# Last tile of an output projection summed from two banks, and two products of an up-projection made in halves of columns

## The chip, the core and the metric

The kernel is one program on one core of a Trainium2 chip. The metric is the device time of one execution in microseconds (us). TensorE (PE) multiplies matrices; VectorE (DVE), ScalarE (ACT) and GpSimd (POOL) work element by element; SyncE (SP) issues the transfers. Each engine has a queue of its own and works through it in order, and waits where an operand is not there yet. TensorE's results land in PSUM, which is cut into banks of 512 float32 columns.

## What is computed

One decoder layer, for 1024 tokens of width 1024, in float32:

```python
h = x * (1.0 + sc1) + sh1
proj = h @ w_in[l]
...                                    # two kinds of attention heads, fox and ret
mix = jnp.concatenate([fox, ret], axis=-1) @ w_out[l]
x = layer_norm(ALPHA * x + g1 * mix, ln1_g[l], ln1_b[l])
h = x * (1.0 + sc2) + sh2
u = causal_depthwise_conv(h @ w_up[l], conv_w[l], conv_b[l])
a, bv = jnp.split(u, 2, axis=-1)
y = (jax.nn.gelu(a, approximate=False) * bv) @ w_down[l]
x = layer_norm(ALPHA * x + g2 * y, ln2_g[l], ln2_b[l])
```

The change lies where the output projection (`w_out`) and its normalisation end and the up-projection (`w_up`, to 2 x 2816 columns) begins.

## The kernel before

Every float32 operand of a large product is kept as a high part (rounded to the format that TensorE reads) and a low part (the rest); a product of two of them is three matmuls: high by high, high by low, low by high (`three`, lines 189 to 191 in the output projection, and `three_w`, lines 1175 to 1177). A split is a cast on ScalarE and a subtraction on VectorE (`op_split_cols`, lines 874 and 875; `w_split`, lines 1124 and 1125).

**Output projection.** The tokens are 8 tiles of 128. For each tile `op_mm` makes 1024 output columns in two halves `n` of 512, from 8 pieces of 128 inputs in two calls (`m4` = 1 for the retention heads, then 0): 12 matmuls for each half and call. The result `op` is one tile of two banks (`bank2`). `op_end` then takes, half by half, `t = op * gate` (line 996) and `acc = ALPHA * x + t` with its row sum (line 997), then the mean (line 1002), the sum of squares on ScalarE (line 1007), its root, the reciprocal, and the normalisation on ScalarE (line 1011). `h2_turn` transposes a finished tile on TensorE (`nT`, line 890), and ScalarE scales it into `hr` (line 893). For the last tile, 7, `op_mm(NT - 1, 0, ...)` has the transposes of tile 6 in its middle, and `op_end` follows.

**Up-projection.** The tokens are parted into even and odd tiles, so that four tiles side by side are 512 columns, and the 1024 inputs into two halves. Of each block `ff` (22 of them, 128 + 128 output rows) 7 products are made in place of 8 (a Strassen-like scheme): products 1 to 7, each of 4 pieces of 128 by 512 columns, thus 12 matmuls. Their operands are `hr` itself and sums of parts of it, `t1` to `t4` (the tile name `ht` in the trace; `h` for the others), made by `h2_sums` (lines 915 to 920) and split by `h2_split`. Columns 0:128 belong to tiles 0 and 1, 128:256 to tiles 2 and 3, 256:384 to tiles 4 and 5, 384:512 to tiles 6 and 7. So the last 128 columns of every operand that mixes even and odd tiles wait for tile 7's normalisation, its transposes, the sums and the splits. The columns 0:384 of `t2` and `t1` are split ahead of that.

`up_12` makes products 1 and 2 (which read even tiles only), `up_657` products 6, 5 and 7, `up_43` products 4 and 3. Product 1 goes into a bank `uX`, is copied out (`u`, line 1190), and products 6, 7 and 4 are added on top in the same bank; product 6's running sum is copied as U2. Product 2 has one bank of `uY`, products 5 and 3 share the other. Weight operands are split as well: `wA` for products 1 and 2, `wS` for 5 and 6, `wD` for 7 and 4, `wZ` for 3. In the program's text the start of the stage reads:

```python
    with tc.issue_after(pins["norm"].ins), tc.issue_after(pins["bias"].ins):
        h2_split("t1", slice(0, 3 * P))
        up_12(0)
        w_s(0, "S")
        h2_turn(NT - 1)
        h2_low(NT - 1)
        for key in ("t2", "t1"):
            low = h2_split(key, slice(3 * P, 4 * P))
        with tc.issue_after(low.ins):
            up_12(1)
```

and then `up_657(0)`, with `up_43(0)` behind it.

**What sets the order.** The text is not the order of the queues. The block is planned when the program is built: of the instructions that are ready in the planner's own model of time, each engine takes the one that stands first in the text. `tc.issue_after(i)` adds that what is written under it comes behind instruction `i` on `i`'s engine. Tiles come out of rings: single banks out of a ring of four ("B"), two-bank tiles out of a ring of two ("A"). A tile that takes a ring's place waits until the one before it there has been read.

Of the kernel before, what the change touches and what calls it, by code (L numbers as in the profile page):

```python
# [8 lines left out]
F32 = mybir.dt.float32  # L9
# [6 lines left out]
P = 128  # L16
# [15 lines left out]
def kernel(  # L32
# [838 lines left out]

    def op_split_cols(key, c, src, sl):
        hi, lo = hop[key][0][c][:, :, sl], hop[key][1][c][:, :, sl]
        nc.scalar.copy(hi, src[:, :, sl])
        return nc.vector.tensor_tensor(out=lo, in0=src[:, :, sl], in1=f(hi), op=ALU.subtract)

    def h2_turn(i):
        n, q0 = i % 2, (i // 2) * P
        acc = accs[i]
        if i < 2:  # L880
            for jp in range(4):
                hr[jp, n] = slot("X", [P, 2, 512], F32, f"hr{jp}_{n}")
        if i == 0:
            op_tiles("11", "X")
            op_tiles("21", "X")
        for q in range(2):
            pt = bank(f"nT{i}_{q}")
            for b in range(4):
                j = 4 * q + b
                nc.tensor.transpose(pt[:, b * P:(b + 1) * P], acc[:, j * P:(j + 1) * P], ident)  # L890
            for b in range(4):
                j = 4 * q + b
                nc.scalar.activation(
                    hr[j // 2, n][:, j % 2, q0:q0 + P], pt[:, b * P:(b + 1) * P], AF.Identity,
                    scale=AB[:, 0, j:j + 1], bias=AB[:, 1, j:j + 1],
                )
            if n == 0:
# [10 lines left out]

    def h2_sums(sl):

        for c in range(2):
            op_split_cols("22", c, hr[2 + c, 1], sl)
            e1, o1 = hr[c, 0][:, :, sl], hr[c, 1][:, :, sl]
            e2, o2 = hr[2 + c, 0][:, :, sl], hr[2 + c, 1][:, :, sl]
            nc.vector.tensor_tensor(out=e1, in0=e1, in1=o1, op=ALU.subtract)
            nc.vector.scalar_tensor_tensor(
                out=o1, in0=o1, scalar=-1.0, in1=o2, op0=ALU.mult, op1=ALU.add)
            nc.vector.scalar_tensor_tensor(
                out=o2, in0=e1, scalar=-1.0, in1=o2, op0=ALU.mult, op1=ALU.subtract)
            nc.vector.scalar_tensor_tensor(  # L920
                out=e2, in0=o2, scalar=-1.0, in1=e2, op0=ALU.mult, op1=ALU.subtract)
# [3 lines left out]
    def h2_split(key, sl):  # L925
        jp, n = TOPS[key]
        if key not in hop:
            op_tiles(key, "H")
        for c in range(2):
            low = op_split_cols(key, c, hr[jp + c, n], sl)  # L930
        return low
# [46 lines left out]
    def op_mm(i, m4, mid=None):  # L978
        if m4 == 1:
            ops[i] = bank2(f"op{i}")  # L980
        s_ = mxs[i, m4]
        for n in range(2):
            sl = slice(n * 512, (n + 1) * 512)
            for m in range(4 * m4, 4 * m4 + 4):
                if mid is not None and n == 0 and m == 4 * m4 + 2:
                    mid()
                three(ops[i][:, sl], s_[:, 0, m % 4, :], s_[:, 1, m % 4, :],
                      wo[m][0][:, sl], wo[m][1][:, sl], m == 4, m == 3)

    def op_end(i):  # L990

        acc, t_ = accs[i], sos[i][:, 512:1024]
        sums = small([P, 2], f"osum{i}")
        for n in range(2):
            sl = slice(n * 512, (n + 1) * 512)
            nc.vector.tensor_tensor(out=t_, in0=ops[i][:, sl], in1=g_row[:, sl], op=ALU.mult)
            pins["sum"] = nc.vector.scalar_tensor_tensor(
                out=acc[:, sl], in0=acc[:, sl], scalar=ALPHA, in1=t_,
                op0=ALU.mult, op1=ALU.add, accum_out=sums[:, n:n + 1],
            )  # L1000
        nmu = small([P, 1], f"onm{i}")
        nc.vector.tensor_scalar(
            out=nmu, in0=sums[:, 0:1], scalar1=sums[:, 1:2], scalar2=-1.0 / D,
            op0=ALU.add, op1=ALU.mult,
        )
        r = small([P, 1], f"ors{i}")
        nc.scalar.activation(sos[i], acc, AF.Square, bias=nmu, accum_out=r)
        nc.scalar.activation(r, r, AF.Sqrt, scale=1.0 / D, bias=epsc)
        nc.vector.reciprocal(r, r)
# [84 lines left out]
    for i in range(NT - 1):  # L1094
        op_mm(i, 0)
        op_split(i + 1, 0)
        if i + 2 < NT:
            x_load(i + 2)
            op_load(i + 2)
            op_split(i + 2, 1)  # L1100
        op_end(i)
        if i > 0:
            h2_turn(i - 1)
            h2_low(i - 1)
            op_mm(i + 1, 1)

# [14 lines left out]
    def w_split(raw, tag, name):  # L1121
        hi = slot(tag, [P, ND, P], F32R, f"{name}h")
        lo = slot(tag, [P, ND, P], F32R, f"{name}l")
        nc.scalar.copy(hi, raw)
        nc.vector.tensor_tensor(out=lo, in0=raw, in1=f(hi), op=ALU.subtract)
        return [(hi[:, k:k + 4, :], lo[:, k:k + 4, :]) for k in (0, 4)]

# [16 lines left out]
    def w_d(ff, tag="X"):

        if ff < NFF:
            a, b = ra[ff], rb[ff]
            nc.vector.tensor_tensor(out=b[:, 0:4, :], in0=a[:, 0:4, :], in1=b[:, 0:4, :],
                                    op=ALU.add)
            W[ff, 7], W[ff, 4] = w_split(b, tag, f"wD{ff}")  # L1150

    def w_4(ff, tag="S"):

        if ff < NFF:
            a, s = ra[ff], rs[ff]
# [36 lines left out]

    def up_12(ff):
        if ff == NFF:
            return
        st = ups[ff] = {"X": bank(f"uX{ff}"), "YZ": bank2(f"uY{ff}")}
        y = st["YZ"][:, 0:512]
        prod(ff, 1, st["X"], True, False)
        s1 = snap(st["X"], f"u1_{ff}")
        prod(ff, 2, y, True, True)  # L1200
        st["a"] = slot("VM", [P, S], F32, f"ua{ff}")
        nc.vector.tensor_tensor(out=rows(st["a"], 0), in0=four(y), in1=four(s1), op=ALU.add)
# [58 lines left out]

    w_load(0, 0)
# [4 lines left out]
    op_mm(NT - 1, 0, lambda: h2_turn(NT - 2))  # L1267
    op_end(NT - 1)
# [3 lines left out]

    with tc.issue_after(pins["norm"].ins), tc.issue_after(pins["bias"].ins):
# [344 lines left out]
```

## Time and profile before

| | us |
|---|---|
| three runs | 1235.55, 1231.77, 1231.75 |
| median | 1231.77 |
| profiled execution | 1230.62 |
| its span (first to last instruction) | 1228.9 |
| TensorE busy in it | 1202.9 |
| VectorE busy | 906.2 |
| ScalarE busy | 651.4 |

All rows further down are of the profiled execution, in us from the start of its span. An instruction stands with its start, its duration, its engine, its line, and output and inputs by the program's names without their numbers; in square brackets stands how long the engine had idled before it, and what released it. Matmuls overlap: one of 512 columns is shown with 0.39 us, but the next can start earlier, so their cost is read from the distance of their starts. PEld is TensorE loading weights. The granted clock (PEclk) is a share of TensorE's full clock, 2.4 GHz; it has one other level, 1.2 GHz.

### The profile page before, as it was taken

To read this page: it belongs to the slowest core of one execution; us is meant where nothing else is said; L and a number is where in the kernel's file an instruction comes from. 1 tells how busy PE (TensorE), PEld (TensorE's weight loads), DVE (VectorE), ACT (ScalarE), POOL (GpSimd) and SP (SyncE) were. 2 spreads that over 40 slices of the span, in tenths; PEclk is the share of its full clock that TensorE was granted. 3 is DMA by queue.
4 is the path that set the end of the run, shared out by engine and by line. 5 is a ranking of instruction groups with operands and counts; after the bars stand their busy time and mean duration, and the time that the engine had idled before them with its cause. 6 is when DMAs were issued, how large, how long until landed. Compare 5 with 4: busy or idle time off the path is not lost.

```text
span 1228.9 us, 17048 instructions
## 1 busy us (share of the span) xinstructions
PE 1202.9 (98%) x5981; PEld 1002.7 (82%) x5981; DVE 906.2 (74%) x1743; ACT 651.4 (53%) x1193; POOL 241.9 (20%) x280
## 2 busy tenths in 40 slices
PE   8999999999999998999899999999999999999997
PEld 6788888898888886788788888888888878888885
DVE  7857656666777778556997787877877875886586
ACT  5635334345666768467765454444544564643452
POOL 0025334213333335100003232121010010000021
PEclk9999999999999999999999999999999999999999
DMA  9523354613352506213169787786444588975751
GB/s 355 223 86 128 114 164 124 211 36 105 103 156 77 174 23 233 94 52 137 52 176 212 194 191 177 205 198 163 129 138 145 154 244 267 322 234 198 257 183 69
DMA packets 86214, 199.78 MB, mean 163 GB/s; under 512 B 9888, under 2 KB 16240, under 8 KB 86128
## 3 DMA queue, kind: packets, MB, share of 16 engines
q1 hardware_dynamic: 73456, 175.62, 41.4%
q0 software_dynamic: 12672, 23.07, 11.8%
q8 instruction: 47, 0.77, 0.3%
q14 instruction: 39, 0.32, 0.1%
HBM read 165.06 MB, written 68.20 MB: 190 GB/s over the span
## 4 chain that ended last, share of the span: by engine, by line
PE 77%; DVE 8%; DMA 7%; ACT 3%; issue 2%; POOL 2%; SPq 0%; DVEq 0%; POOLq 0%; ACTq 0%
PE dX L1359 10%; PE dZ L1359 7%; PE uX L1176 6%; PE uX L1175 6%; PE uX L1177 6%; PE uY L1177 4%; PE uY L1176 4%; PE uY L1175 4%; PE rp L152 4%; PE vp L152 4%; DMA ada<-in_ada_dram 3%; PE pv L845 3%; PE qk L761 2%; PE qk L762 2%; PE qk L763 2%
## 5 line engine op out<-in xcount | busy, mean ns | idle before, releaser
L152 PE MATMUL rp<-wr,hhi 128*128 128x512 f32 x400 | 127.9, 401 | 0.0
L1336 ACT CAST dh<-dr 128x1024 fp32r<-128x1024 f32 x66 | 67.9, 1050 | 77.7 <-DMA dr<-in_w_down_dram 36.0
L1348 DVE TENSOR_TENSOR dl<-dr,dh 128x1024 fp32r<-128x1024 f32 x66 | 80.1, 1237 | 37.4 <-ACT dh L1336 36.3
L807 POOL TENSOR_TENSOR S<-S,dn 128x128 f32<-128x128 f32 (+3 forms) x64 | 74.1, 1163 | 151.5 <-DVE dn L806 125.8
L1022 POOL DMA_DIRECT2D sd<-gd x22 | 18.1, 824 | 392.9 <-DMA sd<-y 227.6
L152 PEld LDWEIGHTS rp<-wr,hhi 128*128 128x128 f32 x400 | 71.6, 189 | 12.7
L152 PE MATMUL rp<-wr,hlo 128*128 128x512 f32 x200 | 78.6, 393 | 0.0
L1359 PE MATMUL dX<-dl,dh 128*128 128x512 f32 x176 | 68.5, 389 | 0.0
L1359 PE MATMUL dX<-dh 128*128 128x512 f32 x176 | 68.5, 389 | 0.0
L1359 PE MATMUL dX<-dh,dl 128*128 128x512 f32 x176 | 68.5, 389 | 0.0
L1190 ACT COPY u<-uX 128x512 f32<-128x512 f32 x44 | 25.8, 587 | 73.6 <-PE uX L1177 73.6
L152 DVE CUSTOM_DVE_ANT_0 ada<-ada,csb,bcol 128x1024 f32<-128x1024 f32 x46 | 59.5, 1298 | 3.4 <-DMA ada<-in_ada_dram 3.4
L803 ACT ACTIVATE S<-S,mn 128x128 f32<-128x128 f32 (+3 forms) x64 | 49.9, 779 | 15.1 <-DVE mn L798 13.9
L761 PE MATMUL qk<-hhi,wqh 128*128 128x512 f32 x128 | 54.6, 427 | 0.0
L836 DVE TENSOR_TENSOR pt<-pt,pt 128x512 fp32r<-128x512 f32 (+2 forms) x96 | 50.8, 550 | 4.3 <-ACT pt L835 3.1
L798 DVE CUSTOM_DVE_ANT_0 S<-ps,nb 128x128 f32<-128x128 f32 (+3 forms) x64 | 48.0, 751 | 8.0 <-PE ps L796 5.6
L845 PE MATMUL pv<-pt,V 128*128 128x256 f32 x320 | 49.9, 293 | 2.4 <-DVE pt L836 1.2
L190 PE MATMUL op<-wol,mxs 128*128 128x512 f32 x128 | 50.4, 394 | 1.7 <-DVE wol L945 1.5
L189 PE MATMUL op<-woh,mxs 128*128 128x512 f32 x128 | 50.8, 398 | 0.9 <-DVE mn L798 0.9
L763 PE MATMUL qk<-hhi,wql 128*128 128x512 f32 x128 | 51.7, 404 | 0.0
L1359 PE MATMUL dZ<-dh 128*128 128x512 f32 x132 | 51.6, 391 | 0.0
L1359 PE MATMUL dZ<-dl,dh 128*128 128x512 f32 x132 | 51.4, 389 | 0.0
(1046 smaller groups left out, 3653.1 us busy)
## 6 DMA issues: line engine op xcount, KB each, us to landing
ada<-in_ada_dram SPq DMA_DIRECT2D x48, 512.0 KB, 3.7
td<-in_w_down_dram SPq DMA_DIRECT2D x44, 256.0 KB, 5.6
wa<-in_w_up_dram SPq DMA_DIRECT2D x22, 512.0 KB, 4.8
wb<-in_w_up_dram SPq DMA_DIRECT2D x22, 512.0 KB, 4.1
gd<-y SPq DMA_DIRECT2D x22, 512.0 KB, 2.9
sd<-y SPq DMA_DIRECT2D x44, 256.0 KB, 3.2
dr<-sd SPq DMA_DIRECT2D x44, 256.0 KB, 3.9
dr<-td SPq DMA_DIRECT2D x44, 256.0 KB, 4.2
```

The source lines that it names most:

```text
L152: order[key] = fn(*args, **kw)
L189: mm(pt, ahi, whi, start=start, stop=False)
L761: nc.tensor.matmul(pt, whi[:, j, :], hhi[j][:, sl], start=(j == 0), stop=False)
L763: nc.tensor.matmul(pt, wlo[:, j, :], hhi[j][:, sl], start=False, stop=(j == ND - 1))
L807: nc.gpsimd.tensor_tensor(out=Ssb[:, :span], in0=Ssb[:, :span], in1=den.to_broadcast([P, span]), op=ALU.mult,)
L845: nc.tensor.matmul(pv[:, :256], V2[h][:, kb, :], pts[kb // 4][u][:, kb % 4, :], start=(kb == 0 and u == 0), stop=(kb == nkb - 1 and u == 1),)
L1175: nc.tensor.matmul(pt, whi, bh, start=start, stop=False, skip_group_check=True)
L1176: nc.tensor.matmul(pt, whi, bl, start=False, stop=False, skip_group_check=True)
L1177: nc.tensor.matmul(pt, wlo, bh, start=False, stop=stop, skip_group_check=True)
L1336: nc.scalar.copy(hi, raw)
L1348: nc.vector.tensor_tensor(out=lo, in0=raw, in1=f(hi), op=ALU.subtract)
L1359: nc.tensor.matmul(pt, w_[:, 0, q], m_[:, 1, :], start=start and n_ == 0, stop=stop and n_ == 2, skip_group_check=True)
```

## The change

The last tile's projection goes into two tiles of one bank each instead of one tile of two, and `op_end` is cut into `op_sum` (one half), `op_mean` and `op_norm`; for tile 7 the sum of half 0 is written between the two halves' matmuls. Products 6 and 5 of the first block are made in two halves of 256 columns: `up_65(0, 0)` makes columns 0:256 and is written behind the splits of the last 128 columns and ahead of `up_12(1)`; `up_657(0)` makes columns 256:512. The other blocks go as before. The rest of the diff cuts functions into smaller ones that issue the same instructions (`op_split_cols`, `h2_turn`, `h2_sums`, `h2_split`, `w_split`, `w_s`, `up_12`) and moves the loop over tiles 0 to 6 behind the definitions, and so behind two sign flips of convolution weights (line 1111).

```diff
-    def op_mm(i, m4, mid=None):
+    def op_half(i, m4, n, mid=None):
+        s_ = mxs[i, m4]
+        sl = slice(n * 512, (n + 1) * 512)
+        for m in range(4 * m4, 4 * m4 + 4):
+            if mid is not None and m == 4 * m4 + 2:
+                mid()
+            three(ops[i][n], s_[:, 0, m % 4, :], s_[:, 1, m % 4, :],
+                  wo[m][0][:, sl], wo[m][1][:, sl], m == 4, m == 3)
+
+    def op_mm(i, m4):
         if m4 == 1:
-            ops[i] = bank2(f"op{i}")
...
+            if i == NT - 1:
+                ops[i] = [bank(f"op{i}_{n}") for n in range(2)]
+            else:
+                pt = bank2(f"op{i}")
+                ops[i] = [pt[:, :512], pt[:, 512:]]
         for n in range(2):
...
+            op_half(i, m4, n)
...
+    def op_sum(i, n):
...
+        nc.vector.tensor_tensor(out=t_, in0=ops[i][n], in1=g_row[:, sl], op=ALU.mult)
+        pins["sum"] = nc.vector.scalar_tensor_tensor(out=acc[:, sl], in0=acc[:, sl], scalar=ALPHA, in1=t_,
+            op0=ALU.mult, op1=ALU.add, accum_out=osum[i][:, n:n + 1])
...
+    def op_end(i):
+        for n in range(2):
+            op_sum(i, n)
+        op_mean(i)
+        op_norm(i)
...
-    def prod(ff, p, pt, start, stop):
-        whi, wlo = W.pop((ff, p))
+    def prod(ff, p, pt, start, stop, sl=slice(0, 512)):
+        whi, wlo = W[ff, p]
...
-            bh, bl = b[0][j // 2][:, j % 2, :], b[1][j // 2][:, j % 2, :]
+            bh, bl = b[0][j // 2][:, j % 2, sl], b[1][j // 2][:, j % 2, sl]
...
+    def up_65(ff, n):
+
+        st, sl = ups[ff], slice(256 * n, 256 * n + 256)
+        prod(ff, 6, st["X"][:, sl], False, False, sl)
+        prod(ff, 5, st["YZ"][:, 512:1024][:, sl], n == 0, False, sl)
+
     def up_657(ff):
         st = ups[ff]
         x_, z = st["X"], st["YZ"][:, 512:1024]
-        prod(ff, 6, x_, False, False)
+        sl = slice(256 if ff == 0 else 0, 512)
+        prod(ff, 6, x_[:, sl], False, False, sl)
         st["U2"] = snap(x_, f"u2_{ff}")
-        prod(ff, 5, z, True, False)
+        prod(ff, 5, z[:, sl], ff > 0, False, sl)
...
-    op_mm(NT - 1, 0, lambda: h2_turn(NT - 2))
-    op_end(NT - 1)
+    nT = []
+    op_half(NT - 1, 0, 0, lambda: h2_turn(NT - 2))
+    op_sum(NT - 1, 0)
+    op_half(NT - 1, 0, 1)
+    op_sum(NT - 1, 1)
+    op_mean(NT - 1)
+    op_norm(NT - 1)
...
             low = h2_split(key, slice(3 * P, 4 * P))
+        up_65(0, 0)
         with tc.issue_after(low.ins):
             up_12(1)
```

## Rows read from the trace of the kernel before

**Rows 1.** The profile page, part 1: busy us of each engine, its share of the span, and its instructions.

```profile
PE 1202.9 (98%) x5981; PEld 1002.7 (82%) x5981; DVE 906.2 (74%) x1743; ACT 651.4 (53%) x1193; POOL 241.9 (20%) x280
```

**Rows 2.** The waits of TensorE: who waited for whom, us in total, times, longest us.

```profile
PE uY L1175 <- ACT ht L874: 2.6, 1, 2.6
...
PE uX L1175 <- DVE ub L1213: 0.5, 1, 0.5
```

**Rows 3.** A table by stretches: from and to, length, then busy us (and instructions) of PE, PEld, DVE, ACT and POOL, the granted clock, the DMA share and GB/s.

```profile
487.40:491.00 3.60, 3.59 (x17) 3.00 (x18) 3.60 (x6) 1.66 (x4) 3.60 (x2) 1.00 0.03 13
...
250.00:277.00 27.00, 27.00 (x225) 26.76 (x224) 17.35 (x87) 12.22 (x54) 4.86 (x8) 1.00 0.07 21
583.80:595.50 11.70, 11.70 (x57) 9.64 (x55) 11.53 (x22) 8.33 (x14) 0.00 (x0) 1.00 0.12 47
595.50:600.20 4.70, 1.24 (x4) 0.37 (x2) 4.70 (x14) 4.70 (x14) 0.00 (x0) 1.00 0.37 113
600.20:604.00 3.80, 3.76 (x10) 2.94 (x11) 3.80 (x7) 1.90 (x3) 0.00 (x0) 0.55 0.07 8
604.00:607.00 3.00, 3.00 (x15) 2.48 (x14) 1.44 (x3) 2.35 (x3) 0.00 (x0) 1.00 0.46 165
```

**Rows 4.** TensorE in order of time, from the last tile's projection (`op`) to product 7 of the first block (`uX` from `wD0h`).

```profile
580.82 0.39 PE L191 MATMUL op<-woh,mxs 128*128 128x512 f32 x1
...
583.78 0.39 PE L1175 MATMUL uX<-h,wA0h 128*128 128x512 f32 x1
...
591.95 1.03 PE L890 MATMUL nT<-ident,acc 128*128 128x128 f32 x8
592.74 0.48 PE L1175 MATMUL uX<-h,wA1h 128*128 128x512 f32 x1
...
595.35 0.39 PE L1177 MATMUL uX<-h,wA1l 128*128 128x512 f32 x1
598.34 0.50 PE L1175 MATMUL uY<-ht,wS0h 128*128 128x512 f32 x1 [2.60 <-ACT ht L874]
599.43 0.51 PE L1175 MATMUL uX<-ht,wS0h 128*128 128x512 f32 x1 [0.59 <-ACT ht L874]
600.24 0.55 PE L1176 MATMUL uX<-ht,wS0h 128*128 128x512 f32 x1 [0.30 <-DVE ht L875]
600.59 0.63 PE L1177 MATMUL uX<-ht,wS0l 128*128 128x512 f32 x1
...
603.15 0.63 PE L1177 MATMUL uX<-ht,wS0l 128*128 128x512 f32 x1
...
606.95 0.39 PE L1175 MATMUL uX<-ht,wD0h 128*128 128x512 f32 x1
607.18 0.39 PE L1176 MATMUL uX<-ht,wD0h 128*128 128x512 f32 x1
```

**Rows 5.** The chain of waits that ended last, two of its pieces in this stage: start, us on the chain, what.

```profile
584.26 0.70 DVE so L996
...
600.24 0.55 PE uX L1176
```

**Rows 6.** VectorE in order of time around the stage.

```profile
583.58 0.76 DVE L875 TENSOR_TENSOR h<-hr,h 128x256 fp32r<-128x256 f32 x2 [1.25 <-ACT h L874]
...
585.71 0.69 DVE L996 TENSOR_TENSOR so<-op,g_row 128x512 f32<-128x512 f32 x1
...
594.32 1.22 DVE L1125 TENSOR_TENSOR wS0l<-ws,wS0h 128x1024 fp32r<-128x1024 f32 x1
...
602.85 1.22 DVE L875 TENSOR_TENSOR ht<-hr,ht 128x1024 fp32r<-128x1024 f32 x1
603.98 0.69 DVE L1160 TENSOR_TENSOR wZ<-wa,wZ 128x512 fp32r<-128x512 f32 x1
606.22 2.36 DVE L875 TENSOR_TENSOR ht<-hr,ht 128x1024 fp32r<-128x1024 f32 x2 [1.56 <-ACT ht L874]
...
612.64 1.22 DVE L1125 TENSOR_TENSOR wS1l<-ws,wS1h 128x1024 fp32r<-128x1024 f32 x1
```

**Rows 7.** All engines in order of time at the end of tile 6's projection: the last matmul of its first half, the last of its second, and its first sum.

```profile
567.97 0.39 PE L191 MATMUL op<-woh,mxs 128*128 128x512 f32 x1
...
570.68 0.40 PE L191 MATMUL op<-woh,mxs 128*128 128x512 f32 x1
...
571.12 0.69 DVE L996 TENSOR_TENSOR so<-op,g_row 128x512 f32<-128x512 f32 x1 [2.22 <-PE op L191]
```

**Rows 8.** TensorE in order of time in an earlier stage whose matmuls have 256 columns; between the two rows stand eleven more of them.

```profile
261.76 0.28 PE L152 MATMUL vp<-wv,hlo 128*128 128x256 f32 x1
...
263.20 0.28 PE L152 MATMUL vp<-wv,hlo 128*128 128x256 f32 x1
```

**Rows 9.** TensorE in order of time, a wait in an earlier stage.

```profile
487.41 0.50 PE L190 MATMUL op<-wol,mxs 128*128 128x512 f32 x1 [1.13 <-DVE wol L945]
```

**Rows 10.** ScalarE in order of time: the cast of wZ, the copy of U2 and the casts of `t3` behind it.

```profile
601.43 0.67 ACT L1159 CAST wZ<-wa 128x512 fp32r<-128x512 f32 x1
604.65 0.59 ACT L1190 COPY u<-uX 128x512 f32<-128x512 f32 x1 [2.56 <-PE uX L1177]
605.14 2.00 ACT L874 CAST ht<-hr 128x1024 fp32r<-128x1024 f32 x2
```

**Rows 11.** TensorE in order of time: the first matmul that reads the low part of the second block's `wS`.

```profile
615.57 0.39 PE L1177 MATMUL uX<-ht,wS1l 128*128 128x512 f32 x1
```

More of the change, by code (lines that the diff above doesn't have):

```diff
@@ L885, in h2_turn, with h2_pe, h2_out @@
             op_tiles("21", "X")
-        for q in range(2):
[L887 to L897, printed above, removed]
+    def h2_pe(i, q):
+        pt = bank(f"nT{i}_{q}")
+        for b in range(4):
+            j = 4 * q + b
+            nc.tensor.transpose(pt[:, b * P:(b + 1) * P], accs[i][:, j * P:(j + 1) * P],
+               ident)
+        return pt
+    def h2_out(i, q, pt):
+        n, q0 = i % 2, (i // 2) * P
+        for b in range(4):
+            j = 4 * q + b
+            nc.scalar.activation(
+                hr[j // 2, n][:, j % 2, q0:q0 + P], pt[:, b * P:(b + 1) * P], AF.Identity,
+                scale=AB[:, 0, j:j + 1], bias=AB[:, 1, j:j + 1],
+            )
+    def h2_turn(i):
+        h2_tiles(i)
+        for q in range(2):
+            h2_out(i, q, h2_pe(i, q))
+            if i % 2 == 0:
+                q0 = (i // 2) * P
                 for c in range(2):
@@ L907, in h2_low, with h2_part, h2_sum1, h2_sum3 @@
             h2_sums(slice(i // 2 * P, i // 2 * P + P))
+    def h2_part(c, sl):
+        return [hr[j, n][:, :, sl] for j in (c, 2 + c) for n in range(2)]
+    def h2_sum1(c, sl):
+        e1, o1, e2, o2 = h2_part(c, sl)
+        nc.vector.tensor_tensor(out=e1, in0=e1, in1=o1, op=ALU.subtract)
+    def h2_sum3(c, sl):
+        e1, o1, e2, o2 = h2_part(c, sl)
+        nc.vector.scalar_tensor_tensor(out=o1, in0=o1, scalar=-1.0, in1=o2, op0=ALU.mult, op1=ALU.add)
+    def h2_sum2(c, sl):
+        e1, o1, e2, o2 = h2_part(c, sl)
+        nc.vector.scalar_tensor_tensor(out=o2, in0=e1, scalar=-1.0, in1=o2, op0=ALU.mult, op1=ALU.subtract)
+    def h2_sum4(c, sl):
+        e1, o1, e2, o2 = h2_part(c, sl)
+        nc.vector.scalar_tensor_tensor(out=e2, in0=o2, scalar=-1.0, in1=e2, op0=ALU.mult, op1=ALU.subtract)
     def h2_sums(sl):
@@ L912, in h2_sums, with top_hi @@
             op_split_cols("22", c, hr[2 + c, 1], sl)
[L913 to L921, printed above, removed]
+            for step in (h2_sum1, h2_sum3, h2_sum2, h2_sum4):
+                step(c, sl)
     TOPS = {"t1": (0, 0), "t2": (2, 1), "t3": (0, 1), "t4": (2, 0)}
-    def h2_split(key, sl):
+    def top_hi(key, c, sl):
         jp, n = TOPS[key]
@@ L928, in h2_split, with top_lo @@
             op_tiles(key, "H")
+        cols_hi(key, c, hr[jp + c, n], sl)
+    def top_lo(key, c, sl):
+        jp, n = TOPS[key]
+        return cols_lo(key, c, hr[jp + c, n], sl)
+    def h2_split(key, sl):
         for c in range(2):
-            low = op_split_cols(key, c, hr[jp + c, n], sl)
+            top_hi(key, c, sl)
+            low = top_lo(key, c, sl)
         return low
@@ L990, in op_end @@
-    def op_end(i):
-        acc, t_ = accs[i], sos[i][:, 512:1024]
[L993 to L1007, printed above, removed]
+    def op_half(i, m4, n, mid=None):
[6 more added lines that the diff above has]
+                  wo[m][0][:, sl], wo[m][1][:, sl], m == 4, m == 3)
@@ L1008, in op_end, with op_mean, op_norm @@
+    def op_mean(i):
+        nmu = osum[i, "nmu"] = small([P, 1], f"onm{i}")
+        sums = osum[i]
+        nc.vector.tensor_scalar(out=nmu, in0=sums[:, 0:1], scalar1=sums[:, 1:2], scalar2=-1.0 / D,
+            op0=ALU.add, op1=ALU.mult)
+        r = osum[i, "r"] = small([P, 1], f"ors{i}")
+        nc.scalar.activation(sos[i], accs[i], AF.Square, bias=nmu, accum_out=r)
         nc.scalar.activation(r, r, AF.Sqrt, scale=1.0 / D, bias=epsc)
+    def op_norm(i):
+        acc, r, nmu = accs[i], osum[i, "r"], osum[i, "nmu"]
@@ L1092 @@
             op_split(0, 0)
[L1094 to L1105, printed above, removed]
     cwv = cw[:, NFF:, :].rearrange("p (k t) c -> p k t c", t=2)
@@ L1191, in snap, with up_banks, up_y @@
         return t
+    def up_banks(ff):
+        ups[ff] = {"X": bank(f"uX{ff}"), "YZ": bank2(f"uY{ff}")}
+    def up_y(ff):
+        st = ups[ff]
+        st["a"] = slot("VM", [P, S], F32, f"ua{ff}")
+        nc.vector.tensor_tensor(out=rows(st["a"], 0), in0=four(st["YZ"][:, 0:512]),
+            in1=four(st["s1"]), op=ALU.add)
     def up_12(ff):
@@ L1195, in up_12 @@
             return
-        st = ups[ff] = {"X": bank(f"uX{ff}"), "YZ": bank2(f"uY{ff}")}
-        y = st["YZ"][:, 0:512]
+        up_banks(ff)
+        st = ups[ff]
         prod(ff, 1, st["X"], True, False)
[L1199 to L1202, printed above, removed]
+        st["s1"] = snap(st["X"], f"u1_{ff}")
+        prod(ff, 2, st["YZ"][:, 0:512], True, True)
+        up_y(ff)
+    def up_65(ff, n):
+        st, sl = ups[ff], slice(256 * n, 256 * n + 256)
+        prod(ff, 6, st["X"][:, sl], False, False, sl)
+        prod(ff, 5, st["YZ"][:, 512:1024][:, sl], n == 0, False, sl)
     def up_657(ff):
@@ L1260, in geglu @@
                         add_to(td[m, q], wdq[0, q][:, 512:1024] if src is None else td[src, q])
+    for i in range(NT - 1):
+        op_mm(i, 0)
+        op_split(i + 1, 0)
+        if i + 2 < NT:
+            x_load(i + 2)
+            op_load(i + 2)
+            op_split(i + 2, 1)
+        op_end(i)
+        if i > 0:
+            h2_turn(i - 1)
+            h2_low(i - 1)
+            op_mm(i + 1, 1)
     w_load(0, 0)
```

56 lines of the change are left out of this document (31 added, 25 removed).

## The prediction

> **What bounds the kernel now.** I read first the shares of the engines: TensorE is busy 98% of the span [rows 1], so a gain can come only from the few places where it waits or runs slow. Second, TensorE's waits, longest first: behind the first stage the longest is 2.6 us, in uY's group at line 1175, for a ScalarE cast of `ht` (the operands t1 and t2 of the up-projection) [rows 2]. That is the place that the change touches. Third, a table by stretches [rows 3]: TensorE is full from 583.8 to 595.5, busy 1.24 of the next 4.70 us, granted 0.55 of its clock from 600.2 to 604.0, and full at 1.00 afterwards. Fourth, TensorE in order of time [rows 4]: the last product before the gap starts at 595.35; one matmul of product 5 follows at 598.34 and one of product 6 at 599.43, each released by a cast; at 600.24 the low parts are there and the rest runs on. From 600.59 to 603.15 six matmuls of 512 columns take 2.56 us, 0.427 each, against (591.95 - 583.78)/36 = 0.227 before the gap: that is the 1.2 GHz level, after 2.60 us of idling and two short waits. Products 6 and 5 are over when product 7 starts at 606.95. Without wait and slow clock their 24 matmuls would have ended at 595.57 + 24 x 0.227 = 601.0. **The prize of this place is 5.9 us**, 0.48% of the time; nothing in the change touches another wait of TensorE.
>
> Fifth, the chain of waits: in this stage it lies on VectorE, from the sum of the last tile at 584.26 until the split of `ht` that lets TensorE start at 600.24 [rows 5]. VectorE is full from 583.80 on but for 0.17 us [rows 3], and idles only before it, 1.25 us ahead of 583.58 [rows 6], and behind it. So VectorE's work, more than the normalisation's latency, dates the end of the gap.
>
> **The change part by part.**
>
> *Two banks for the last tile.* It removes the wait of the first half's sum for the second half's matmuls. That there is one is seen on tile 6: its first half ended with the matmul at 567.97, yet the sum started at 571.12, right behind the last matmul at 570.68, after 2.22 us of idling [rows 7]. For tile 7 the first half ends with the matmul at 580.82 (+0.39), the second where the next product starts, at 583.78 [rows 4]. The sum of a half is two VectorE instructions; two halves start 585.71 - 584.26 = 1.45 us apart [rows 5, 6]. The first half's 1.45 us can lie between 581.2 and 584.26, where VectorE has two pairs of splits and idles 1.25 us ahead of the second pair [rows 6], and a little more before the first. I take it that all of it is hidden there: the second half's sum then takes the place at 584.26, and mean, square, root, normalisation and everything queued behind them on VectorE move up by 1.45 us. Bounds: 0 (the planner gives the idle time to something else, or a split slips by as much) and 1.45. Where it goes wrong the splits of `h` are late: product 1 of the up-projection needs them from 584 on, so a slip is paid on TensorE at the same rate, and no more than the 1.45 us. The new banks come out of the ring of four single banks: the first product's bank is then the one that held the first half, and waits for its multiplication, due about 583, ahead of 583.78. Cost nothing while the sum is early; up to 1 us if it is not. The moved loop puts two small sign flips earlier and costs nothing: they depend on weights loaded long before.
>
> *Products 6 and 5 of the first block in two halves of columns.* The 24 matmuls of 512 columns become 48 of 256. Twelve matmuls of 256 columns between 261.76 and 263.20 take 1.44 us, 0.120 each [rows 8], so the split costs 24 x (2 x 0.120 - 0.227) = 0.31 us of TensorE, with 24 more weight loads inside that spacing. The clock is 1.00 over a stretch of such matmuls from 250 to 277 [rows 3]. The Trainium skill (TensorE: Matmul & The Clock Gate, Back-to-back issue gap) gives a warm matmul N/2.4 + 2.5 ns, 109 and 216 ns for these widths; by that the split would cost 24 x 2.6 ns = 0.06 us. The rows are some 10 ns above both figures, so I keep 0.31. What it buys: the first half needs only the tokens of tiles 0 to 3, and their parts of t1 and t2 are split from tiles 0 to 5 ahead of the last tile. TensorE has from 583.78: 48 matmuls of the two first blocks (10.9 us), the transposes of tile 7 (592.74 - 591.95 = 0.79) and now 24 half matmuls (2.88), to 598.35 instead of 595.57. The weight split they need ended at 594.32 + 1.22 = 595.54 [rows 6], so even on the old times it is not late.
>
> *Where the gap goes.* The second half waits for the same split of `ht` as before, 600.24 [rows 5], 1.45 us earlier: 598.79. TensorE idles 0.4 us instead of 2.6 and more, and the clock should hold: after a wait of 1.13 us at 487.41 [rows 9] the next stretch was granted 1.00 [rows 3]. The second half takes 2.88 us, to 601.67, **5.28 us ahead** of 606.95.
>
> *What is late next.* Product 7's second matmul, at 607.18 before [rows 4], needs the low part of the first piece of t3, which VectorE ends at 602.85 + 1.22 = 604.07 [rows 6]; 1.45 earlier is 602.62, behind TensorE. So 4.55 us are left. Its seventh and eighth matmul need the second piece of t3. Before, VectorE waited 1.56 us for that cast at 606.22 [rows 6], because ScalarE had the copy of U2 ahead of it and stood 2.56 us for TensorE [rows 10]. Now U2 is there near 600.3, while ScalarE is busy with wZ until about 602.1 - 1.45 = 600.65, so copy and cast end by 602.2; VectorE reaches that split behind wZ's, at 604.67 - 1.45 = 603.2, and ends it near 604.4. TensorE would want it at 602.65 + 6 x 0.227 = 604.0. Another 0.35 us: **4.2 us are left**. VectorE is now 606.22 - 603.2 = 3.0 us ahead of its old times, and works back to back until wS1l, 612.64 + 1.22 = 613.86 [rows 6], now 610.85. The first matmul on it stood at 615.57 [rows 11], now 611.37: 0.5 us of slack. A gain above 4.7 us would be cut there. Behind it TensorE is full at 1.00 with splits many us ahead, so the lead is carried to the end.
>
> *Sum.* -5.9 (gap and slow clock) + 0.31 (halves) + 0.4 (wait left) gives the 5.28; + 0.73 and 0.35 for VectorE under product 7 gives **-4.2 us**. The profiled execution took 1230.62 and would take 1226.4; the median shown, 1231.77, lies 1.15 above it and becomes **1227.6**.
>
> **The rivals.**
>
> *A, half the mechanism (1229.0).* The early sum moves nothing, as VectorE's time before 584.26 is taken. Then product 7's second matmul stands at 604.07, and with the second piece of t3 2.75 us are left. For it: the order of each queue is planned anew. Against it: the idle 1.25 us in the row. If instead the early sum works and the halves do not, the gap only moves up by 1.45: 1230.3. The two hold 0.30.
>
> *B, more (1226.2).* The planner orders VectorE's work so that t3 is no brake: 5.28, or 5.6 with no wait left. The slack at wS1l speaks against more than 4.7 unless that work moves too. 0.12.
>
> *C, slower (1233.2).* The 24 half matmuls stand ahead of the second block's 24 in the program. If they also stand ahead of them in TensorE's queue, TensorE reaches them behind the transposes, near 592, and waits for wS0's split until about 595.5 [rows 6], with 24 full matmuls queued behind that did not wait before. The wait is as long as the old one and brings the low clock again, which cost 8 x 0.2 = 1.6 us and a little at its ends. From 595.5: 2.88 + 24 x 0.227 + 2.88 and 1.7 is 608.4, 1.45 us slower than 606.95 where the sum is not early either, and even where it is. The point from which it decides: 12 of the 24 behind the halves give 605.7, still faster; some 18 give no change. Against it: before, the planner put product 2 of that block ahead of the transposes. 0.09.
>
> *D, the rest planned otherwise (above 1235.5).* If the new order costs each of 21 blocks a wait like the 0.5 us for `ub` [rows 2], 10 us come on top; from eight such waits on the gain is gone. Nothing in the rows asks for it. 0.06.
>
> **How the numbers follow.** Forecast 0.43, A 0.30, B 0.12, C 0.09, D 0.06. About 0.3% (3.7 us) is what a measurement of this kernel can tell from no change, so faster means below 1228.1. The forecast's own range is 1226.4 (from the profiled execution) to 1229.0; some four fifths of it lie below the bound. That and B give faster 0.46; A, C and the rest of the forecast give same 0.48; D slower 0.06. The range starts at 1230.62 - 5.6 = 1225.0 and reaches past A to 1232.0, short of C and D.
>
> **What the changed profile would show.** Right: 24 more matmuls; a sum of the last tile near 582 and the second near 584.3; TensorE's waits in this stage under 1.5 us together; granted clock 1.00 from 595 to 607; 256-column matmuls 0.120 apart; product 7 starting near 601.7 and held by VectorE's split of `ht`; its first matmul of block 1's product 6 near 610.9. Wrong: both sums behind 584 (A); a wait over 2 us ahead of the first half matmul and a clock near 0.5 (C); TensorE waits in later blocks (D). If the gap closes but the end does not come earlier, the carrying of the lead was wrong.

## The result and the profile after

The changed kernel takes **1226.55 us** (median of 6 runs, 1225.6 to 1227.6) beside 1232.2 us for the kernel before on the same chip (6 runs): ratio 0.995, 95% interval 0.9937 to 0.9963. A second comparison gave 1225.93 (5 runs) beside 1230.92: 0.9959, interval 0.9947 to 0.9971. Faster by 5.0 to 5.7 us, by the medians; the forecast was 1227.6. Two executions of variants below, of 3113 and 1495 us, stand far from all others of their kernels; they count in no ratio and move the medians given by 0.15 us at most.

The profiled execution took 1225.86 us with a span of 1224.2. The page's first part answers to [rows 1]: 24 more matmuls, as the halving demands, and TensorE still at 98%.

```profile
PE 1201.2 (98%) x6005; PEld 1002.8 (82%) x6005; DVE 905.6 (74%) x1743; ACT 651.3 (53%) x1193; POOL 241.7 (20%) x280
```

TensorE's waits (total, times, longest). The 2.6 us for the cast of `ht` [rows 2] are gone. From product 1 on two waits remain; the one for `ub` was there before, and the one for a split of `ht` is new.

```profile
PE uX L1226 <- DVE ht L877: 0.8, 1, 0.8
...
PE uX L1225 <- DVE ub L1278: 0.5, 1, 0.5
```

The table by stretches, three of those in [rows 3] (length, busy us and instructions of PE, PEld, DVE, ACT, POOL, granted clock, DMA share, GB/s). TensorE is busy 4.69 us of the 4.70 in which it was busy 1.24, and the stretch that was granted 0.55 is at 1.00.

```profile
583.80:595.50 11.70, 11.70 (x66) 10.09 (x65) 11.50 (x20) 9.79 (x19) 0.00 (x0) 1.00 0.17 58
595.50:600.20 4.70, 4.69 (x33) 4.19 (x32) 4.68 (x13) 4.52 (x10) 0.00 (x0) 1.00 0.21 86
600.20:604.00 3.80, 2.97 (x17) 2.38 (x16) 3.80 (x5) 3.80 (x6) 0.00 (x0) 1.00 0.39 117
```

TensorE in order of time, against [rows 4, 11]: the first product; tile 7's transposes; the first half matmul of product 6, and the first that reads the low part of `wS0`; the second half's start and the matmul that the first of the last splits releases; the last half matmul; product 7's first and second; the first of the second block's product 6, and the first on `wS1l`.

```profile
583.24 0.39 PE L1225 MATMUL uX<-h,wA0h 128*128 128x512 f32 x1
...
590.05 1.04 PE L896 MATMUL nT<-ident,acc 128*128 128x128 f32 x8
...
592.29 0.28 PE L1225 MATMUL uX<-ht,wS0h 128*128 128x256 f32 x1
...
593.93 0.28 PE L1227 MATMUL uX<-ht,wS0l 128*128 128x256 f32 x1
...
597.94 0.28 PE L1225 MATMUL uX<-ht,wS0h 128*128 128x256 f32 x1
...
598.35 0.39 PE L1226 MATMUL uX<-ht,wS0h 128*128 128x256 f32 x1
...
600.96 0.28 PE L1227 MATMUL uY<-ht,wS0l 128*128 128x256 f32 x1
601.08 0.39 PE L1225 MATMUL uX<-ht,wD0h 128*128 128x512 f32 x1
602.30 0.50 PE L1226 MATMUL uX<-ht,wD0h 128*128 128x512 f32 x1 [0.83 <-DVE ht L877]
...
610.37 0.39 PE L1225 MATMUL uX<-ht,wS1h 128*128 128x512 f32 x1
...
610.83 0.39 PE L1227 MATMUL uX<-ht,wS1l 128*128 128x512 f32 x1
```

The whole stage starts 0.54 us earlier (583.24 for 583.78), so every time below is counted from product 1's first matmul:

| from product 1's first matmul, us | before | after | earlier by | forecast |
|---|---|---|---|---|
| transposes of tile 7 | 8.17 | 6.81 | 1.36 | 1.45 |
| first matmul that the last splits of `ht` release | 16.46 | 15.11 | 1.35 | 1.45 |
| product 7, first matmul | 23.17 | 17.84 | 5.33 | 5.28 |
| product 7, second matmul | 23.40 | 19.06 | 4.34 | 4.55 |
| second block, first matmul on `wS1l` | 31.79 | 27.59 | 4.20 | 4.2 |
| down-projection, first matmul | 423.14 | 418.99 | 4.15 | 4.2 |

The chain of waits that ended last, two pieces that answer to [rows 5] (start, us on the chain, what). It still lies on VectorE from the last tile's second sum, but now it goes back to TensorE only at product 7's second matmul.

```profile
583.79 0.61 DVE so L1042
...
602.30 0.50 PE uX L1226
```

VectorE in order of time, against [rows 6]: the first half's sum (580.70 and 581.97) lies around a pair of splits of `h`, and 0.37 us of the idle 1.25 is left.

```profile
580.70 0.69 DVE L1042 TENSOR_TENSOR so<-op,g_row 128x512 f32<-128x512 f32 x1
581.30 0.75 DVE L877 TENSOR_TENSOR h<-hr,h 128x256 fp32r<-128x256 f32 x2
581.97 0.68 DVE L1043 SCALAR_TENSOR_TENSOR acc<-acc,so 128x512 f32<-128x512 f32 x1
...
583.03 0.76 DVE L877 TENSOR_TENSOR h<-hr,h 128x256 fp32r<-128x256 f32 x2 [0.37 <-ACT h L873]
583.71 0.68 DVE L1042 TENSOR_TENSOR so<-op,g_row 128x512 f32<-128x512 f32 x1
...
592.31 1.21 DVE L1169 TENSOR_TENSOR wS0l<-ws,wS0h 128x1024 fp32r<-128x1024 f32 x1
...
601.03 2.35 DVE L877 TENSOR_TENSOR ht<-hr,ht 128x1024 fp32r<-128x1024 f32 x2
603.30 0.69 DVE L1210 TENSOR_TENSOR wZ<-wa,wZ 128x512 fp32r<-128x512 f32 x1
...
609.30 1.23 DVE L1169 TENSOR_TENSOR wS1l<-ws,wS1h 128x1024 fp32r<-128x1024 f32 x1
```

ScalarE, against [rows 10]: U2's copy no longer waits 2.56 us for TensorE, and the cast of `t3`'s second piece follows at 600.75.

```profile
600.27 0.58 ACT L1240 COPY u<-uX 128x512 f32<-128x512 f32 x1
600.75 1.05 ACT L873 CAST ht<-hr 128x1024 fp32r<-128x1024 f32 x1
```

So 4.20 of the 4.7 us between the two spans come from the stage, and the down-projection starts with 4.15 of it. The other 0.54 us lie ahead of the stage: TensorE's first matmul of the output projection already stands at 478.35 for 478.87. A second profile of the changed kernel starts the stage at 582.66, and gives 4.19 for it. Variants that share the changed code begin it between 582.96 and 584.11, the old code at 583.78 and 583.80. Whether a part of this early lead belongs to the change stays open; nothing below rests on it.

### The profile page after: what moved, and what is told of

The parts are those of the page before. It is cut to its first block, busy times and chain, and to the rows that moved or that the text cites. A ratio compares the mean times of both kernels' runs of the same rounds, so it can differ in the third digit from the quotient of the medians.

```text
span 1224.2 us, 17091 instructions
## 1 busy us (share of the span) xinstructions
PE 1201.2 (98%) x6005; PEld 1002.8 (82%) x6005; DVE 905.6 (74%) x1743; ACT 651.3 (53%) x1193; POOL 241.7 (20%) x280
## 4 chain that ended last, share of the span: by engine, by line
PE 78%; DVE 8%; DMA 7%; ACT 3%; issue 2%; POOL 2%; SPq 0%; DVEq 0%; POOLq 0%; ACTq 0%
PE dX L1443 10%; PE dZ L1443 7%; PE uX L1226 6%; PE uX L1225 6%; PE uX L1227 6%; PE rp L152 4%; PE uY L1225 4%; PE uY L1227 4%; PE uY L1226 4%; PE vp L152 4%; DMA ada<-in_ada_dram 3%; PE pv L845 3%; PE qk L761 2%; PE qk L762 2%; PE qk L763 2%
## 5 line engine op out<-in xcount | busy, mean ns | idle before, releaser
L1443 PE MATMUL dZ<-dh,dl 128*128 128x512 f32 x132 | 51.4, 389 | 0.0
```

The source lines that it names most:

```text
L1443: nc.tensor.matmul(pt, w_[:, 0, q], m_[:, 1, :], start=start and n_ == 0, stop=stop and n_ == 2, skip_group_check=True)
```

## The experiments

Theory: the early sum moves VectorE's queue up by some 1.4 us, the halves fill TensorE's wait, both together keep the clock, and VectorE's splits of `t3` and `wS1` end the gain. Rivals: one part alone does it all; the slow clock had another cause than the idling; the halving costs next to nothing. **The stage** below is the time from product 1's first matmul in block 0 to product 6's first in block 1: 31.33 us before, 27.13 after. Diffs are against the changed kernel unless another is named.

**The early sum alone.** Products 6 and 5 in one piece, as before.

```
-        sl = slice(256 if ff == 0 else 0, 512)
+        sl = slice(0, 512)
...
-        prod(ff, 5, z[:, sl], ff > 0, False, sl)
+        prod(ff, 5, z[:, sl], True, False, sl)
...
-        up_65(0, 0)
```

> The changed kernel with products 6 and 5 of the first block whole again: the two banks and the early sum alone. Theory: VectorE's chain is 1.45 us earlier, so the splits that release TensorE come 1.45 us earlier and TensorE idles some 1.3 us instead of 2.6 before its next matmul. If such a short wait leaves the clock at 1.00, the slow stretch (1.6 us) is gone as well: 3.0 us faster than before, about 0.25%, VectorE's split of t3 not late. If the low clock comes all the same: 1.45 us faster. Rival (the early sum moves nothing, the halves do all): no difference from before, wait 2.6 us and clock 0.55.

Measured: 1229.16 us beside 1231.26, ratio 0.998 (0.9971 to 0.999); stage 28.41, a gain of 2.92. TensorE's waits in the gap, product 7, and, 400 us later, a new wait in the last block:

```profile
596.09 0.50 PE L1225 MATMUL uY<-ht,wS0h 128*128 128x512 f32 x1 [1.14 <-ACT ht L873]
597.22 0.49 PE L1225 MATMUL uX<-ht,wS0h 128*128 128x512 f32 x1 [0.63 <-ACT ht L873]
598.12 0.50 PE L1226 MATMUL uX<-ht,wS0h 128*128 128x512 f32 x1 [0.41 <-DVE ht L877]
...
603.26 0.39 PE L1225 MATMUL uX<-ht,wD0h 128*128 128x512 f32 x1
...
1001.63 0.50 PE L1225 MATMUL uY<-h,wZ 128*128 128x512 f32 x1 [1.09 <-ACT u L1240]
```

The stretch that had 0.55 of the clock (columns as in the tables above):

```profile
600.20:604.00 3.80, 3.80 (x19) 3.13 (x18) 3.80 (x5) 3.02 (x5) 0.00 (x0) 1.00 0.45 138
```

What follows: the gap shrinks by what VectorE moved up, and what is left of it no longer costs the clock. So the early sum alone is worth more than its own 1.35 us. It kept less of that: the down-projection starts only 1.66 us earlier (421.48 after product 1 for 423.14), as the whole queue was planned anew and the last block got the wait of 1.09. That is rival D's kind of loss in one block.

**The halves alone.** The last tile in two neighbouring banks again, both sums behind both halves.

```
-            if i == NT - 1:
-                ops[i] = [bank(f"op{i}_{n}") for n in range(2)]
-            else:
-                pt = bank2(f"op{i}")
-                ops[i] = [pt[:, :512], pt[:, 512:]]
+            pt = bank2(f"op{i}")
+            ops[i] = [pt[:, :512], pt[:, 512:]]
...
-    op_sum(NT - 1, 0)
     op_half(NT - 1, 0, 1)
+    op_sum(NT - 1, 0)
     op_sum(NT - 1, 1)
```

> The changed kernel with the last tile in one tile of two banks and both sums behind the matmuls, as before: the halves alone. Theory: the half products fill 2.9 us of the gap, the second half still waits for VectorE's split at the old time (1.8 us of idling), the clock stays at 1.00, and product 7's second matmul waits for VectorE's split of t3 at the old time: 2.75 to 3.1 us faster than before. Rival (the early sum does nothing): 4.2 us faster, as with both. With the early sum alone near 3.0 and the halves alone near 2.9 the two do not add up to the 4.2 of both, since VectorE ends the stage.

Measured: 1227.65 us beside 1231.26, ratio 0.9971 (0.9961 to 0.9982). The trace is that of a second run of the same kernel, at 1227.62:

> The halves alone once more, for a trace. Stage (before 31.33, both 27.13): 28.3 to 28.6 if product 7 waits for VectorE's split at its old place, with TensorE idling some 1.8 us ahead of the second half products and the clock at 1.00 or near it; 29.8 or more if the low clock comes back.

Its stage takes 28.52, a gain of 2.81. TensorE in order of time: the two waits at the second half, then product 7.

```profile
599.55 0.39 PE L1222 MATMUL uX<-ht,wS0h 128*128 128x256 f32 x1 [0.86 <-ACT ht L873]
600.13 0.39 PE L1223 MATMUL uX<-ht,wS0h 128*128 128x256 f32 x1 [0.19 <-DVE ht L877]
...
602.87 0.39 PE L1222 MATMUL uX<-ht,wD0h 128*128 128x512 f32 x1
604.15 0.50 PE L1223 MATMUL uX<-ht,wD0h 128*128 128x512 f32 x1 [0.89 <-DVE ht L877]
```

What follows: product 7 is reached 4.00 us earlier (602.87 - 583.70 = 19.17 for 23.17), but its second matmul only 2.95 (20.45 for 23.40): VectorE's split of `t3` stands about where it stood (it starts at 602.88, 19.18 after product 1, for 19.07), and holds TensorE. The two parts are therefore neither alternatives nor a sum: 2.92 + 2.81 is 1.5 more than 4.20. Both take the same wait and both save the same clock, and the early sum moves the brake behind the halves by 1.39 (20.45 for 19.06).

The same trace shows in which order the halves ran here. VectorE's split of `wS0`, and the first matmul that reads it:

```profile
594.22 1.22 DVE L1166 TENSOR_TENSOR wS0l<-ws,wS0h 128x1024 fp32r<-128x1024 f32 x1
...
595.79 0.27 PE L1224 MATMUL uX<-ht,wS0l 128*128 128x256 f32 x1
```

The split ended at 595.44, at its old place after product 1 (11.74 for 11.76), and still nothing waited for it.

**Twelve useless matmuls in the old gap.** The kernel before, with 12 more matmuls of 512 columns behind the second block's products 1 and 2 and ahead of product 5, into a bank that product 5 then starts anew. Against the kernel before:

```
+        for _ in range(12):
+            nc.tensor.matmul(ups[0]["YZ"][:, 512:1024], hop["11"][0][0][:, 0, 0:P],
+                             hop["11"][0][0][:, 0, :], start=True, stop=True, ...)
```

> The kernel before with twelve extra matmuls of 512 columns that compute nothing that is used, placed in TensorE's queue where it idled 2.6 us. Theory: the slow stretch came from that idle time, so with the gap filled to about 598.3 the clock stays at 1.00 and the 24 matmuls end some 1.6 us earlier, though the splits come at the old time: 1.6 us faster than before, granted clock 1.00 from 600.2 to 604.0. Rival (the clock falls there for another reason, or the wait alone was the loss): no difference, clock near 0.55.

Measured: 1228.71 us beside 1231.26, ratio 0.9983 (0.9974 to 0.9992), with more work. The stage takes 29.71, 1.62 less than before. The filler, the two short waits that are left (the second for the low parts), and product 7:

```profile
595.57 2.88 PE L1284 MATMUL uY<-h 128*128 128x512 f32 x12
...
599.42 0.49 PE L1175 MATMUL uX<-ht,wS0h 128*128 128x512 f32 x1 [0.59 <-ACT ht L874]
600.23 0.50 PE L1176 MATMUL uX<-ht,wS0h 128*128 128x512 f32 x1 [0.31 <-DVE ht L875]
...
605.35 0.39 PE L1175 MATMUL uX<-ht,wD0h 128*128 128x512 f32 x1
```

And the stretch with the slow clock:

```profile
600.20:604.00 3.80, 3.77 (x17) 3.12 (x18) 3.80 (x7) 2.83 (x5) 0.00 (x0) 1.00 0.11 9
```

What follows: the splits came at the old time (600.23 for 600.24), so nothing was gained in the gap itself; product 7 starts 1.60 earlier because the 24 matmuls run at the 2.4 GHz level. The two short waits (0.59 and 0.31) are still there, so they alone do not bring the slow clock; without the 2.60 us of idling ahead of them it did not come, and **1.6 us of the 5.9 were clock**. With that, the early sum's 2.92 is about 1.35 + 1.6.

**Every block in halves.** All 22 blocks split products 6 and 5 as block 0 does.

```
         sl = slice(256 if ff == 0 else 0, 512)
+        if ff > 0:
+            up_65(ff, 0)
+        sl = slice(256, 512)
...
-        prod(ff, 5, z[:, sl], ff > 0, False, sl)
+        prod(ff, 5, z[:, sl], False, False, sl)
```

> The changed kernel with products 6 and 5 of all 22 blocks made in halves of 256 columns, where the other 21 blocks had no wait to fill: 504 more matmuls. It prices the halving by itself. By the rows (0.120 us for 256 columns, 0.227 for 512): 21 x 0.31 = 6.5 us slower than the changed kernel, so about 1.5 us slower than the kernel before. Rival, the skill page's formula (2.6 ns a matmul): 1.3 us slower than the changed kernel. Rival, the clock falls under the narrow matmuls: some tens of us slower.

Measured: 1236.67 us beside 1231.26, ratio 1.0043 (1.0029 to 1.0057): 5.4 us slower than the kernel before where 1.5 was expected, and some 10 us over the changed kernel. The price of the halving came as expected. From block 5's product 6 to block 10's: 96.90 us for 95.20, or **0.34 us for each block**, against the 0.31 that the rows of an earlier stage had given and the 0.06 of the formula in the Trainium skill (TensorE: Matmul & The Clock Gate, Back-to-back issue gap), where it is given for an isolated matmul. 21 blocks make 7.1 us. What the expectation lacked lies in the last block, where a new wait is followed by slow matmuls, 0.427 apart ((1010.69 - 1008.13)/6):

```profile
1007.02 0.50 PE L1225 MATMUL uX<-ht,wD21h 128*128 128x512 f32 x1 [3.40 <-ACT u L1240]
...
1008.13 0.63 PE L1226 MATMUL uX<-ht,wD21h 128*128 128x512 f32 x1
...
1010.69 0.63 PE L1226 MATMUL uX<-ht,wD21h 128*128 128x512 f32 x1
```

The granted clock is 0.66 from 1007 to 1012: the matmuls between 1007.81 and 1011.46 take 3.65 us for 9 x 0.227 = 2.04, another 1.6 us. Under the narrow matmuls themselves it is 1.00 from 600 to 1000, so the rival of a clock that falls there is out. What follows: the price of the halving is as forecast, and where no wait is to be filled it is a loss.

**Past the brake, three tries.** If VectorE's split of `t3` holds the stage, then to take work out of VectorE's queue ahead of it must bring up to 1.0 us more. One: the split of `wA1` on GpSimd.

```
-    def w_lo(raw, hi, lo):
-        nc.vector.tensor_tensor(out=lo, in0=raw, in1=f(hi), op=ALU.subtract)
+    def w_lo(raw, hi, lo, eng=None):
+        (eng or nc.vector).tensor_tensor(out=lo, in0=raw, in1=f(hi), op=ALU.subtract)
...
-            W[ff, 1], W[ff, 2] = w_split(ra[ff], tag, f"wA{ff}")
+            eng = nc.gpsimd if ff == 1 else None
+            W[ff, 1], W[ff, 2] = w_lo(*w_hi(ra[ff], tag, f"wA{ff}"), eng)
```

> The changed kernel with one split taken off VectorE: the low part of the second block's wA (1.22 us on VectorE, between the last sum and the mean) is made by GpSimd, which does nothing in this stage and needs 2.4 to 3.4 us for that shape. Theory: VectorE ends the stage, so everything behind moves up by 1.14 us, the wait of 0.83 us in product 7 goes, and TensorE, which is then full, can gain no more than that and 0.2 us: stage (first matmul of product 1 to first matmul of the second block's product 6) 27.13 in the changed kernel, now 26.1 to 26.3; 0.8 to 1.0 us faster than the changed kernel. Rival (TensorE's own work or ScalarE ends the stage): 27.1, no difference.

Measured: a miss. 1229.66 beside 1230.92, ratio 0.9986 (0.9978 to 0.9995); stage 30.27, 3.1 *longer* than the changed kernel's. All engines in order of time, three rows:

```profile
585.20 2.40 POOL L1169 TENSOR_TENSOR wA1l<-wa,wA1h 128x1024 fp32r<-128x1024 f32 x1 [89.37 <-ACT wA1h L1165]
585.30 2.85 DVE L1043 SCALAR_TENSOR_TENSOR acc<-acc,so 128x512 f32<-128x512 f32 x1
...
592.49 1.97 PE L896 MATMUL nT<-ident,acc 128*128 128x128 f32 x8 [2.32 <-ACT acc L1059]
```

VectorE's sum of the last tile takes 2.85 us instead of 0.69 while GpSimd runs, and ends 0.55 behind GpSimd's end at 587.60, as if it had been held until then and had run at its usual pace after it. The Trainium skill (SBUF — State Buffer, Who interferes with whom) states that a VectorE instruction with two inputs in SBUF contends with a GpSimd one that reads SBUF, and calls the ports that they share an exclusive lock. The trace agrees, and so does that of the run with both edits (2.85 beside 2.39); the expectation had left it out. It hit the worst place: the normalisation is late, the transposes wait 2.32 us, and the granted clock from 590 to 596 is 0.72; behind the wait, from 592.49 to 596, it is 0.55.

Two: the addition `ua` of the second block placed behind the first piece of `t3`, by a hint to the planner.

```
-        up_y(ff)
+        if ff != 1:
+            up_y(ff)
...
-        h2_split("t3", slice(0, 4 * P))
+        top_hi("t3", 0, slice(0, 4 * P))
+        low3 = top_lo("t3", 0, slice(0, 4 * P))
+        with tc.issue_after(low3.ins):
+            up_y(1)
+        top_hi("t3", 1, slice(0, 4 * P))
+        top_lo("t3", 1, slice(0, 4 * P))
```

> The changed kernel with one VectorE instruction moved, nothing removed: the add of the second block's product 2 (0.68 us) is put behind the split of the first piece of t3, for which product 7 waits 0.83 us. Theory: that wait falls to about 0.15 us, and the second piece's split is no later than its matmul wants it: stage 27.13 becomes 26.4 to 26.7, 0.4 to 0.7 us faster than the changed kernel. Rival (the order of VectorE's work does not matter because ScalarE's casts come too late): 27.1.

Measured: also a miss. 1227.24 beside 1230.92, ratio 0.9972 (0.9963 to 0.9981); stage 28.19, 1.06 longer. TensorE in order of time:

```profile
602.20 0.50 PE L1225 MATMUL uX<-ht,wD0h 128*128 128x512 f32 x1 [0.60 <-ACT u L1240]
...
606.63 0.50 PE L1227 MATMUL uY<-h,wZ 128*128 128x512 f32 x1 [0.97 <-DVE wZ L1210]
```

The wait for `ht` is gone as meant, but the planner put the cast of `t3`'s second piece ahead of U2's copy on ScalarE, which now holds product 7, and wZ's split behind `t4` on VectorE, which holds product 4. ScalarE's cast and copy, which stood the other way round in the changed kernel (600.75 and 600.27):

```profile
600.10 1.04 ACT L873 CAST ht<-hr 128x1024 fp32r<-128x1024 f32 x1
...
601.56 0.58 ACT L1240 COPY u<-uX 128x512 f32<-128x512 f32 x1
```

Both edits together did no better:

> Both edits of the two runs beside it: the low part of wA on GpSimd, and the add behind t3's first split. Theory: TensorE is full as soon as either has taken the 0.83 us away, so the two do not add up: stage 26.1 to 26.3, as with GpSimd alone. Rival (VectorE still holds TensorE up with GpSimd alone): shorter than with GpSimd alone by 0.3 us or more.

Measured: 1230.59 beside 1230.92, ratio 0.9998 (0.999 to 1.0007), stage 31.58, with a wait for the transposes of 2.32 and one for wZ of 1.14. The changed kernel ran beside these three, which is the second comparison given above:

> The changed kernel itself, timed beside the three variants on the same chip so that differences under 1 us can be judged. Expected: ratio to the kernel before 0.995 to 0.997, stage 27.1.

Three: the same idea with the order of these splits written out in the text, behind the copy of U2.

```
-        up_y(ff)
+        if ff != 1:
+            up_y(ff)
...
+        if ff == 0:
+            top_hi("t3", 1, slice(0, 4 * P))
+            top_lo("t3", 1, slice(0, 4 * P))
+            w_4(0)
+            h2_split("t4", slice(0, 4 * P))
+            up_y(1)
...
-        h2_split("t3", slice(0, 4 * P))
-        h2_split("t4", slice(0, 4 * P))
-        w_4(0)
+        top_hi("t3", 0, slice(0, 4 * P))
+        top_lo("t3", 0, slice(0, 4 * P))
```

> The changed kernel with the add of the second block's product 2 behind all splits of t3 and t4 again, but with ScalarE's copy of U2 written ahead of the casts that had got in its way when the add alone was moved (second piece of t3 ahead of it, wZ and t4 behind it); nothing removed. Theory: product 7 waits only for the copy of U2, some 0.3 us later than in the changed kernel, and for no split: its second matmul stands 0.5 to 0.7 us earlier, stage 26.4 to 26.7 against 27.13, 0.4 to 0.7 us faster than the changed kernel. Rival (the time behind product 7 is set by VectorE's total work, the order is worth nothing): 27.1, or more where another split is late.

Measured: 1227.09 beside 1231.61, ratio 0.9965 (0.9953 to 0.9977): not shown different from the changed kernel. The stage takes 26.50, 0.63 less, as expected, but the kernel does not get faster by it. TensorE's second matmul of product 7 no longer waits, but the first on `wS1l` comes right when VectorE has made it:

```profile
601.88 0.39 PE L1226 MATMUL uX<-ht,wD0h 128*128 128x512 f32 x1
...
611.21 0.50 PE L1227 MATMUL uX<-ht,wS1l 128*128 128x512 f32 x1
```

VectorE's row for that split:

```profile
609.93 1.23 DVE L1169 TENSOR_TENSOR wS1l<-ws,wS1h 128x1024 fp32r<-128x1024 f32 x1
```

It ends at 611.16. It also starts later than in the changed kernel (26.48 us after product 1 for 26.06), behind the moved addition and one more, so at the first matmul on `wS1l` the lead is already gone (27.76 for 27.59). It stays gone at the third block's first matmul (35.34 for 35.29), and 0.57 us more go to a wait for U's copy in the last block (at 1000.32). What follows: VectorE's order was the brake at product 7, but the next split stands close behind it. Neither of the two orders tried kept the prize; that no order can is not shown.

## Why the prediction was right

**Mechanism and size held**: a forecast of -4.2 us in the stage, 4.20 measured, and carried to the down-projection. That the two agree to 0.1 us is in part luck, as errors of 0.1 to 0.35 cancel (below). The medians moved by 0.8 to 1.5 us more; the profiles place 0.5 of such a difference ahead of the stage, and the rest is within the spread of the executions (1225.6 to 1227.6 after). The time lies below the 1228.1 from which the prediction counted a change as faster, a case that it gave 0.46 beside 0.48 for one too small to tell.

**The prize of this place.** 5.9 us as the sum of a wait and a slow clock: the useless matmuls return 1.62, near the 1.6 that the eight-matmul estimate in rival C had for the clock. That leaves 4.3 for the wait, by difference.

**Two banks for the last tile.** Forecast 1.45, of a range from 0 to 1.45; measured 1.35 at the second half, 1.28 at the first split of `t3` (601.03 - 583.24 = 17.79 for 602.85 - 583.78 = 19.07). The first half's sum did lie in the idle time that [rows 6] had shown, and the second one took the first's old place, 0.47 after product 1's start for 0.48. The ring of single banks cost nothing: the first half's bank was read by 581.39 (580.70 + 0.69), ahead of product 1 at 583.24.

**Products 6 and 5 in two halves.** 0.120 us apart ((600.96 - 599.76)/10), as in [rows 8]; 0.34 for each block where 0.31 was put. The rows were right, and the formula of the Trainium skill cited above was too low for this stream of matmuls.

**Where the gap goes.** Product 7 came 5.33 us earlier where 5.28 was said. The wait in front of the second half is 0.18 (0.30 from 598.05 to 598.35, less 0.12), for the 0.4 of the forecast. Two small errors met: the second half was released 0.10 later than forecast (15.11 after product 1 for 15.01), but took 2.73 and not 2.88, as two of its 24 matmuls read only high parts and ran ahead of that point. TensorE started the first half before the second block's products were over, at 592.29; it did not wait there, as `wS0l` was split at 593.52 and first read at 593.93. Rival C had feared this order. It cost nothing with the weight split moved up, and nothing in the halves alone, where the split stood at its old place: matmuls on `wA1` and on the high part of `wS0` ran ahead of the first on its low part.

**What is late next.** Here two terms were off and cancelled. Product 7's second matmul lost 0.99 (5.33 - 4.34) and not 0.73, because VectorE moved up by 1.28 and not 1.45. The 0.35 for `t3`'s second piece did not come: VectorE took both pieces back to back, ahead of wZ. Another 0.14 went up to `wS1l`, 0.11 of it right behind the wait, where the next matmul follows after 0.34 (602.30 to 602.64) and not 0.23. At `wS1l` the slack is 0.3 (split over at 610.53, read at 610.83) for the 0.5 of the forecast. The order written by hand ran into that split, which it had itself moved back by 0.42.

**The rivals.** *A* was priced wrong in one of its halves: with the early sum alone "the gap only moves up by 1.45" leaves out that the shorter waits no longer cost the clock, and the stage gained 2.92. Its other half, 2.75 for the halves alone, measured 2.81. *D* did not come in the changed kernel; three variants showed its kind in the last block (1.09, 3.40 and 0.57 us).

## What to carry to other kernels

Look at the engine on which the chain of waits lies before it reaches the stalled one: here 1.35 us of early work on VectorE and columns of a product that were ready already were worth 4.2 us on TensorE together, and either alone less than 3. A short gap on TensorE can cost more than its length (here 1.6 us of slow clock behind 2.60 us of idling), so shortening it can give back more than its length; useless matmuls of the same length, put into the gap, tell the wait and the clock apart. When a planner orders the queues, read the whole trace after an edit, as a gain in one stage was in part lost in another four hundred us later.

## What the runs showed that was not expected

- GpSimd's subtraction of 128x1024 elements (2.40 us) held up a VectorE instruction with two inputs in SBUF: 2.85 us for one of 0.69, in both runs that had it. Moving 1.2 us of work off VectorE made the stage 3.1 us longer.
- Waits of 1.14, 0.63 and 0.41 us left the next stretch at a granted clock of 1.00; one of 2.60 with two short ones behind it had left 0.55, one of 2.32 was followed by 0.55 over 3.5 us, and one of 3.40 by 0.66 over 5 us.
- The same hint to the planner that moved one addition also swapped a cast and a copy on another engine, which cost 0.60 us at product 7.
